# Down products that load the next part's first operand before the evictions, h before its weights, and the last retention transposes one part later

## The chip, the cores and the metric

The kernel runs on one core of one Trainium2 chip. The metric is device time in microseconds (us) of one launch; the figure before is the median of three runs. The profile is one further execution of the same program, so its times are that execution's own.

The engines are named as the profile names them: PE is TensorE (its weight loads are PEld), DVE is VectorE, ACT is ScalarE, POOL is GpSimd, and SP is the queue that issues nearly all DMAs.

## What is computed

The reference is one inference step of a two-layer encoder trunk of width 1024, over 1024 prompt frames and 32 frames of a running stream (1056 columns in all). Cut to what matters:

```python
# layer 0: retention, layer 1: gated linear attention (GLA); each followed by a ConvFFN
x = x + y_mixer          # retention: (silu(g) * o) @ w_out, o normalised per head, K = 2048
h = rmsnorm(x, norm_ffn[i])
u = h @ w_up             # 1024 -> 5632
c = conv over 3 frames of u
x = x + (silu(gate) * val) @ w_down    # K = 2816
```

and at the end a last RMSNorm. All matrices are fp32. The kernel splits each fp32 operand into a high part `hi` (rounded to the fp32r type that TensorE multiplies) and a rest `lo`, and forms each product as three matmuls: hi·hi, hi·lo, lo·hi.

## The kernel before, in words

Most large products (up, most of down, the projections of retention) are done by a seven-product Strassen scheme. What is left to the class `Down` are four plain "down" products, each `out[1024, columns] += W.T @ h` with the residual added:

- `d1r`, layer 0's retention output (`w_ro`, 16 K tiles), in four parts of 264 columns; it reads `scr_o[0]`, which retention has written to memory.
- `d1` of layer 1, GLA's output (`w_go`, 8 K tiles), in four parts of 264 columns.
- `down` of layers 0 and 1, the last 6 K tiles of `w_down` (`NF - NS`), in parts of 384, 384 and 288 columns.

A part c accumulates 8 output tiles nt in 8 PSUM banks (tile `pd`), so that all eight banks are taken while the last K tile is multiplied. For each K tile i, `load(c, kt)` fetches the weights (tile `raw`, then ACT's copy to `whi`, `kw` or `kh` at L104 and DVE's difference to `wlo`, `kw` or `kl`), and the operand h (a DMA into a room `hr`, then ACT's copy to `hh` at L1248 and DVE's difference to `hl` at L1249; in `d1r` and `d1` these rooms lie in the tiles AR and XB, so the trace calls them AR and XB). Weights of the K tiles in `keep` stay on chip for all parts, and a later part begins with them. In the plain `down` of layer 0, K tiles 0 and 1 were split early; their tiles are called `ehi` and `elo`.

After the last K tile of each bank, `evict` adds bank and residual on DVE (L1662 in `d1r`, L1728 in layer 0's `down`), squares the result on ACT (L138) and sums the squares on DVE and POOL (L149). In layer 0's `down` it also makes the next layer's operand, ACT at L153 and DVE at L154 (tile XA). The next part's products need these banks: a bank is free when its eviction has read it. During the first `hold` K tiles J of a new part only 7 of the 8 output tiles are done, so that one bank serves the norm of the part before (`norm_a`, tile `pn`).

Retention's last step, four PE transposes into a PSUM tile `pt` (L831), a product with the gate on DVE (L832) and a store to `scr_o`, is left over as a "tail" and is run by `run_tails` from within `d1r`. Its 32 columns are read by part 3 of `d1r` alone.

The order on each engine is made by a scheduler that goes by the order in which the code is written, by dependences, by its own estimate of times and by when a buffer of a pool comes free. Each engine runs its own list strictly in that order; SP issues its DMAs in its order too, and stands still while the next DMA's room is taken. The kept residual load of a part (`xr`, L1259) is a DMA of 1 MB or more on that queue.

The names that follow: h is the right operand, "residual" is `xr`, "part 0 to part 1" is the change from c = 0 to c = 1.

Of the kernel before, what the change touches and what calls it, by code (L numbers as in the profile page):

```python
# [52 lines left out]
def trunk_kernel(ctx: ExitStack, tc: tile.TileContext, io):  # L53
    nc = tc.nc
# [44 lines left out]
    def load_w(src, dst=None, after=None):  # L99
        i = uid()  # L100
        raw = raw_tile(f"raw{i}")
        nc.sync.dma_start(raw, src)
        hi, lo = dst or (w_tile(f"whi{i}"), w_tile(f"wlo{i}"))
        ins = S.copy(hi, raw), V.tensor_tensor(lo, raw, hi.bitcast(F32), op=ALU.subtract)  # L104
        if after is not None:
            for a, b in zip(ins, after):
                order(a, b)
        return hi, lo
# [3 lines left out]
    def preload(*keys):  # L112
        for k in keys:
            ahead[k] = load_w(io[k[0]][k[1:]])
# [99 lines left out]
    def new_ss(depth=1):  # L214
        return [nps[0].tile([P, 384], F32, tag="ss", name=f"ss{uid()}", bufs=2 * depth) for _ in range(2)]
# [286 lines left out]
    def pairs_phase(cs, SA, sp, UR, NB, gn, xp, finish, then):  # L502
# [77 lines left out]
        def leave(f, s):  # L580
# [7 lines left out]
            else:  # L588
# [5 lines left out]
                nc.sync.dma_start(scr_qk[key[0], key[1], :, :, c0:c0 + n].rearrange("d p t -> p d t"), u)  # L594

        load(0)
        for n, (s, f, i) in enumerate(seven_order(len(todo))):
            m = ORD[i]
            if n in (14, 18):
                t = cs[n // 4 - 3]  # L600
                V.tensor_tensor(t, t, R, op=ALU.mult)
            if s == 0 and i == 2 and f + 1 < len(todo):
                load(f + 1)
            if i == 0:
                unit[f, s] = {}
                U[f, s] = UA.tile([P, 2, 2 * TH], F32, tag="u", name="", bufs=3)

            def put(j, half, op, t, b):
                V.tensor_tensor(U[f, s][:, j, half * TH:half * TH + TH], t, b, op=op)

            seven(m, unit[f, s], W[f], X[s], sm, snap, put)
            if i == 6:
                leave(f, s)
            later(steps, 1)
            if f == len(todo) - 1 and (s, i) in then:
                then[s, i]()
# [11 lines left out]
    def retention(d1):  # L628
# [214 lines left out]
        first_down = []  # L843
        run = chunk(heads[0], 0)
        next(run)
        for n in range(len(units)):
            next(run)
            then = None
            if n + 1 < len(units):
                h, m = units[n + 1]  # L850
                if h not in heads:
                    heads[h] = Head(h)
                then = chunk(heads[h], m)
                next(then)
            next(run)
            if then is None:
                for split in first_down:
                    split()
            if n == len(units) - 4:
                for kt in range(3):  # L860
                    o = RH * P + 16 + kt * D
                    q = RH * P + 16 + 3 * D + kt * TH
                    first_down.append(d1.early(kt, raw_tile("he")[:, :TH] if kt == 2 else early[-1][:, q:q + TH],
                                               early[-1][:, o:o + D]))
            if n in (0, 2):
                refill(n + 1)
            if n == 4:
                xs[0] = sample_x(rp)
            run = then
# [331 lines left out]
    def run_tails(sm):  # L1201
        while tails:
            tails.pop()(sm)

    def later(todo, k):
        for _ in range(min(k, len(todo))):
            todo.pop(0)()
# [3 lines left out]
    class Down:  # L1211
# [23 lines left out]
        def load(self, c, kt):  # L1235
            if (c, kt) in self.ops:
                return
            c0, n = self.chunks[c]
            if kt not in self.keep:
                w = load_w(self.wsrc(kt))  # L1240
            else:
                if kt not in self.kept:
                    self.kept[kt] = load_w(self.wsrc(kt), self.room("kw"))
                w = self.kept[kt]
            hr = self.room("hr")[:, :n]
            nc.sync.dma_start(hr, self.hsrc(kt)[:, c0:c0 + n])
            hh, hl = self.room("hh"), self.room("hl")
            S.copy(hh[:, :n], hr)  # L1248
            V.tensor_tensor(hl[:, :n], hr, hh[:, :n].bitcast(F32), op=ALU.subtract)  # L1249
            self.ops[c, kt] = w, (hh, hl)  # L1250

        def run(self, room, evict, norm_a, norm_b, done, nxt=()):
            self.room = room
            nk, sm, keep = self.nk, self.sm, self.keep
            todo, ss, last = [], None, None
            for c, (c0, n) in enumerate(self.chunks):
                xr = room("xr")[:, :KT * n].rearrange("p (k t) -> p k t", k=KT)
                if c:
                    nc.sync.dma_start(xr, self.res[:, :, c0:c0 + n])  # L1259
                prev, ss = ss, new_ss()  # L1260
                kts = list(range(nk))
                if c:
                    kts = list(keep) + [k for k in kts if k not in keep]
                J = self.hold
                ps, dg = {}, [None]

                def mm(i, nt):
                    if nt not in ps:
                        ps[nt] = sm("pd")
                    k = slice(nt * P, nt * P + P)  # L1270
                    w, h = self.ops[c, kts[i]]
                    o = ps[nt][:, :n]
                    PE.matmul(o, w[0][:, k], h[0][:, :n], start=i == 0, stop=False)  # L1273
                    PE.matmul(o, w[0][:, k], h[1][:, :n], start=False, stop=False)  # L1274
                    self.last_mm = PE.matmul(o, w[1][:, k], h[0][:, :n], start=False, stop=i == nk - 1)  # L1275

                for i, kt in enumerate(kts):
                    self.load(c, kt)
                    if c == 0 and i == 4:
                        nc.sync.dma_start(xr, self.res[:, :, c0:c0 + n])  # L1280
                    if c == len(self.chunks) - 1 and i == nk - 3:
                        preload(*nxt)
                    if c == 0 and i < self.narrow:
                        for nt in range(5):
                            mm(i, nt)
                        continue

                    if c == 0 and i and i == self.narrow:
                        for nt in range(5, KT):
                            for k in range(i):  # L1290
                                mm(k, nt)

                    if prev is None or i > J:
                        for nt in range(KT):
                            mm(i, nt)
                            if i == nk - 1:
                                evict(c, nt, xr[:, nt], ps[nt][:, :n], ss)
                        if c == 0 and i == self.narrow:
                            run_tails(sm)
                        later(todo, 3 if nk > 8 else 6)  # L1300
                        continue

                    if i < J:
                        for nt in range(KT - 1):
                            mm(i, nt)
                        if i == J - 1:
                            dg[0] = norm_a(c - 1, prev)
                    else:
                        first = 5 if norm_b else 3
                        for nt in range(first):  # L1310
                            mm(i, nt)
                        if norm_b:
                            norm_b(c - 1, dg[0])
                        for k in range(J):
                            mm(k, KT - 1)
                        for nt in range(first, KT):
                            mm(i, nt)
                        todo.extend(done(c - 1, last))
                last = xr
            return ss, todo, xr  # L1320
# [594 lines left out]
```

## Time and profile before

| | us |
|---|---|
| median of 3 runs (lowest to highest) | 2878.23 (2876.97 to 2879.57) |
| profiled execution, its own time | 2871.2 |
| its span, first to last instruction | 2869.3 |
| PE busy | 2791.4 (97%) |
| DVE busy | 2145.1 (75%) |
| ACT busy | 1332.3 (46%) |
| POOL busy | 277.8 (10%) |
| `d1r`, from its first product to the start of the last L1273 | 709.5 to 910.0 |
| layer 0's `down`, likewise | 1538.0 to 1619.2 |
| `d1` of layer 1, likewise | 2046.1 to 2144.1 |
| layer 1's `down`, likewise | 2781.1 to 2853.1 |

PE works nearly all the time, so what matters is where it stands still and at what clock it runs. The last four rows are places in the span. The whole program's granted clock is 0.993 of full speed.

### The profile page before, as it was taken

The page shows a single profiled execution, that of the slowest core. Times are in us where ns is not written, and L with a number is a line of the kernel's source. Part 1 is how long each engine was busy: PE and PEld are TensorE (multiplying, and loading weights), DVE is VectorE, ACT ScalarE, POOL GpSimd, SP SyncE. Part 2 cuts the span into 40 slices and gives each one's busy share as a digit, 9 for nine tenths or more (in the row PEclk, how much of TensorE's full clock was granted, in tenths as well). Part 3 has the DMA queues.
Part 4 walks back from the last instruction along what each step waited for, and adds up shares of the span by engine and source line. Part 5 has one row for each costly group of instructions (what it writes and reads, how often), then busy time and mean ns, then how long its engine had stood idle before and what let it go on. Part 6 is the DMA issues. An engine that isn't in the chain of part 4 may idle for free.

```text
span 2869.3 us, 52602 instructions
## 1 busy us (share of the span) xinstructions
PE 2791.4 (97%) x20954; PEld 2687.3 (94%) x20954; DVE 2145.1 (75%) x3529; ACT 1332.3 (46%) x2401; POOL 277.8 (10%) x516
## 2 busy tenths in 40 slices
PE   8999999999999999999999999999998999999998
PEld 8999988788999999999999889999998999999997
DVE  7777777777678887878775577774498788878756
ACT  8433344444444544445443455553254444445434
POOL 1000000000000111111000232220011111110001
PEclk9999999999999999999999999999999999999999
DMA  6333377664765223333867201114642233428663
GB/s 219 106 124 103 128 262 239 199 192 154 260 210 166 82 75 128 121 128 113 286 205 246 90 27 46 51 44 153 222 155 70 75 110 123 143 75 271 210 231 115
DMA packets 234486, 427.22 MB, mean 149 GB/s; under 512 B 27616, under 2 KB 146016, under 8 KB 233216
## 3 DMA queue, kind: packets, MB, share of 16 engines
q1 hardware_dynamic: 233696, 423.27, 44.4%
q8 instruction: 164, 2.69, 0.4%
q14 instruction: 82, 0.67, 0.1%
q10 hardware_dynamic: 544, 0.59, 0.1%
HBM read 299.94 MB, written 123.85 MB: 148 GB/s over the span
## 4 chain that ended last, share of the span: by engine, by line
PE 80%; DVE 9%; DMA 4%; ACT 3%; issue 2%; POOL 1%; SPq 0%; DVEq 0%; ACTq 0%; POOLq 0%
PE pu L333 16%; PE pu L328 16%; PE pu L332 16%; PE pd L1274 3%; PE pd L1275 3%; PE pd L1273 3%; PE psv L233 2%; PE psv L232 2%; PE psv L231 2%; PE pj L124 1%; PE pj L126 1%; PE pj L125 1%; PE pg L124 1%; PE pg L125 1%; PE pg L126 1%
## 5 line engine op out<-in xcount | busy, mean ns | idle before, releaser
L104 DVE TENSOR_TENSOR wlo<-raw,whi 128x1024 fp32r<-128x1024 f32 x161 | 201.3, 1253 | 97.3 <-ACT whi L104 46.0
L1527 ACT COPY AR<-pu 128x264 f32<-128x264 f32 x264 | 99.0, 375 | 303.0 <-PE pu L333 300.3
L104 ACT CAST whi<-raw 128x1024 fp32r<-128x1024 f32 x161 | 167.8, 1047 | 118.4 <-DMA raw<-w_ro 26.7
L333 PE MATMUL pu<-XA,wgl 128*128 128x264 f32 x752 | 213.8, 284 | 0.0
L328 PE MATMUL pu<-XA,wgh 128*128 128x264 f32 x752 | 213.3, 284 | 0.0
L332 PE MATMUL pu<-XA,wgh 128*128 128x264 f32 x752 | 213.2, 283 | 0.0
L1274 PE MATMUL pd<-XB,whi 128*128 128x264 f32 x552 | 158.2, 288 | 2.2 <-DVE XB L1249 2.2
L1549 DVE SCALAR_TENSOR_TENSOR AR<-AR,cw 128x1058 f32<-128x1058 f32 x88 | 115.9, 1318 | 58.5 <-ACT AR L1548 55.9
L1275 PE MATMUL pd<-XB,wlo 128*128 128x264 f32 x552 | 158.3, 288 | 0.0
L1273 PE MATMUL pd<-XB,whi 128*128 128x264 f32 x552 | 154.0, 287 | 0.0
L328 PE MATMUL pu<-XA,wsh 128*128 128x264 f32 x520 | 148.7, 286 | 1.7 <-DVE AR L1523 1.0
L333 PE MATMUL pu<-XA,wsl 128*128 128x264 f32 x520 | 148.6, 286 | 0.8 <-DVE wsl L301 0.8
L332 PE MATMUL pu<-XA,wsh 128*128 128x264 f32 x520 | 147.8, 284 | 0.0
L301 DVE TENSOR_TENSOR wtl<-rv,wth 128x1024 fp32r<-128x1024 f32 x58 | 71.0, 1225 | 101.6 <-ACT wth L300 99.6
L1523 DVE TENSOR_TENSOR AR<-AR,pu 128x264 f32<-128x264 f32 (+2 forms) x440 | 144.6, 368 | 0.0
L328 PEld LDWEIGHTS pu<-XA,wgh 128*128 128x128 f32 x752 | 141.6, 188 | 0.0
L332 PEld LDWEIGHTS pu<-XA,wgh 128*128 128x128 f32 x752 | 141.5, 188 | 0.0
L333 PEld LDWEIGHTS pu<-XA,wgl 128*128 128x128 f32 x752 | 141.4, 188 | 0.0
L328 PE MATMUL pu<-XA,whi 128*128 128x264 f32 x448 | 127.5, 285 | 3.8 <-ACT XA L1418 3.0
L333 PE MATMUL pu<-XA,wlo 128*128 128x264 f32 x448 | 127.3, 286 | 1.5 <-DVE wlo L104 1.5
L332 PE MATMUL pu<-XA,whi 128*128 128x264 f32 x448 | 127.0, 285 | 0.2
L328 PE MATMUL pu<-XA,wth 128*128 128x264 f32 x408 | 116.3, 285 | 0.1
(478 smaller groups left out, 10547.1 us busy)
## 6 DMA issues: line engine op xcount, KB each, us to landing
raw<-w_ro SPq DMA_DIRECT2D x52, 512.0 KB, 4.8
rg<-w_up SPq DMA_DIRECT2D x44, 512.0 KB, 3.6
rv<-w_up SPq DMA_DIRECT2D x44, 512.0 KB, 3.5
scr_h<-AR SPq DMA_DIRECT2D x44, 512.0 KB, 2.7
AR<-scr_x SPq DMA_DIRECT2D x32, 528.0 KB, 4.9
scr_x<-AR SPq DMA_DIRECT2D x32, 528.0 KB, 3.6
raw<-scr_w SPq DMA_DIRECT2D x32, 512.0 KB, 5.2
AR<-scr_h SPq DMA_DIRECT2D x28, 528.0 KB, 4.8
```

Of the source, the lines that this page charges most:

```text
L104: ins = S.copy(hi, raw), V.tensor_tensor(lo, raw, hi.bitcast(F32), op=ALU.subtract)
L124: PE.matmul(ps, hi[:, k], rh, start=kt == 0, stop=False)
L301: V.tensor_tensor(l_, src, h.bitcast(F32), op=ALU.subtract)
L328: mm = PE.matmul(ps, wh[:, k], x[:, 0, kt], start=m in (1, 2, 4, 5) and kt == 0, stop=False, skip_group_check=True)
L332: PE.matmul(ps, wh[:, k], x[:, 1, kt], start=False, stop=False, skip_group_check=True)
L333: mm = PE.matmul(ps, wl[:, k], x[:, 0, kt], start=False, stop=kt == 3, skip_group_check=True)
L1273: PE.matmul(o, w[0][:, k], h[0][:, :n], start=i == 0, stop=False)
L1274: PE.matmul(o, w[0][:, k], h[1][:, :n], start=False, stop=False)
L1275: self.last_mm = PE.matmul(o, w[1][:, k], h[0][:, :n], start=False, stop=i == nk - 1)
L1523: V.tensor_tensor(u[:, d:d + n], t[:, o:o + n], b[:, o:o + n], op=op)
L1527: S.copy(t, b)
L1549: V.scalar_tensor_tensor(cj, uj[:, 1:T + 3], cw[:, nt, 1:2], cj, op0=ALU.mult, op1=ALU.add)
```

## The change

```diff
             c0, n = self.chunks[c]
+            hr = self.room("hr")[:, :n]
+            nc.sync.dma_start(hr, self.hsrc(kt)[:, c0:c0 + n])
             if kt not in self.keep:
                 w = load_w(self.wsrc(kt))
             ...
-            hr = self.room("hr")[:, :n]
-            nc.sync.dma_start(hr, self.hsrc(kt)[:, c0:c0 + n])
             hh, hl = self.room("hh"), self.room("hl")
...
                     self.load(c, kt)
+                    if i == nk - 1 and c + 1 < len(self.chunks):
+                        self.load(c + 1, (list(keep) or [0])[0])
...
-                        if c == 0 and i == self.narrow:
-                            run_tails(sm)
                         later(todo, 3 if nk > 8 else 6)
                         continue
                     if i < J:
                         for nt in range(KT - 1):
                             mm(i, nt)
+                        if c == 1 and i == 1:
+                            run_tails(sm)
```

Three edits, all in `Down`. `load` writes the DMA of h ahead of that of its weights. At the last K tile of a part, `load` of the next part's first K tile (a kept one) is written ahead of that last tile's products and evictions. The tail of retention is run in part 1 after the second K tile, no longer in part 0 after the fourth. Nothing is added or left out: the same instructions stand in another order. The lines below the edits are two higher in the changed kernel (L1662 is L1664 there, L1728 is L1730), and the DMA of h is L1240 there.

PE, `d1r`, end of part 0, before; `pd_7535` is output tile 4 of part 0, `pt_7630` the transposes, `on_7469` retention's last rows:

```order
L1273 MATMUL pd_7535<-XB_7516,whi_7999 128x264
L1274 MATMUL pd_7535<-XB_7516,whi_7999 128x264
L831 MATMUL pt_7630<-ident,on_7469 128x32 x4
L1275 MATMUL pd_7535<-XB_7516,wlo_8000 128x264
L1273 MATMUL pd_7576<-XB_7516,whi_7999 128x264
```

PE in the changed kernel, 52 rows later, after the second K tile of part 1 (`pd_8091` is its output tile 6):

```order
L1273 MATMUL pd_8091<-XB_7516 128x264
L1274 MATMUL pd_8091<-XB_7516 128x264
L1275 MATMUL pd_8091<-XB_7516 128x264
L831 MATMUL pt_8119<-ident,on_7469 128x32 x4
L1273 MATMUL pd_8067<-XB_7516 128x264
```

The transposes stood among the last products of part 0, with ten products of that part behind them; now they stand behind 42 products of part 1.

PE, layer 0's `down`, part 0 to part 1, before; `pd_16844` is the last bank of part 0, `pd_17070` to `pd_17094` are the seven banks of part 1, `hh_17066` and `hl_17067` the two halves of its first h:

```order
L1275 MATMUL pd_16844<-hh_16982,kl_16976 128x384
L1273 MATMUL pd_17070<-hh_17066,ehi_16674 128x384
L1273 MATMUL pd_17074<-hh_17066,ehi_16674 128x384
L1273 MATMUL pd_17078<-hh_17066,ehi_16674 128x384
L1273 MATMUL pd_17082<-hh_17066,ehi_16674 128x384
L1273 MATMUL pd_17086<-hh_17066,ehi_16674 128x384
L1273 MATMUL pd_17090<-hh_17066,ehi_16674 128x384
L1273 MATMUL pd_17094<-hh_17066,ehi_16674 128x384
L1274 MATMUL pd_17070<-hl_17067,ehi_16674 128x384
```

The same place in the changed kernel, where the first h is `hh_16987` and `hl_16988`:

```order
L1275 MATMUL pd_16844<-hh_16982,kl_16977 128x384
L1273 MATMUL pd_17070<-hh_16987,ehi_16674 128x384
L1274 MATMUL pd_17070<-hl_16988,ehi_16674 128x384
L1275 MATMUL pd_17070<-hh_16987,elo_16675 128x384
L1273 MATMUL pd_17074<-hh_16987,ehi_16674 128x384
```

and one K tile on (second h `hh_17099`, `hl_17100`; `pn_17150` is the first matmul of the norm of part 0):

```order
L1273 MATMUL pd_17090<-hh_17099,ehi_16727 128x384
L1273 MATMUL pd_17094<-hh_17099,ehi_16727 128x384
L168 MATMUL pn_17150<-ones,ss_16814 128x1
L1274 MATMUL pd_17070<-hl_17100,ehi_16727 128x384
L1275 MATMUL pd_17070<-hh_17099,elo_16728 128x384
```

Before, the seven products with the rounded half stood first in K tile 0, and those with its rest behind them; now K tile 0 goes bank by bank, and the sorting by halves has moved to K tile 1, with the first matmul of the norm in its middle.

DVE at that place, before (L1728 are evictions 3 to 7, `hl_17067` is the rest of the first h of part 1):

```order
L1728 TENSOR_TENSOR AR_7512<-AR_7512,pd_16828 128x384
L154 SCALAR_TENSOR_TENSOR XA<-AR_7512,gcol,XA 128x384
L1728 TENSOR_TENSOR AR_7512<-AR_7512,pd_16832 128x384
L154 SCALAR_TENSOR_TENSOR XA<-AR_7512,gcol,XA 128x384
L149 TENSOR_TENSOR ss_16814<-ss_16814,sq_17008 128x384
L154 SCALAR_TENSOR_TENSOR XA<-AR_7512,gcol,XA 128x384 x2
L149 TENSOR_TENSOR ss_16814<-ss_16814,sq_17028 128x384
L1728 TENSOR_TENSOR AR_7512<-AR_7512,pd_16836 128x384
L1728 TENSOR_TENSOR AR_7512<-AR_7512,pd_16840 128x384
L1728 TENSOR_TENSOR AR_7512<-AR_7512,pd_16844 128x384
L1249 TENSOR_TENSOR hl_17067<-AR_7512,hh_17066 128x384
```

DVE in the changed kernel, from eviction 3 on (L1730); `hl_16988` now stands ahead of eviction 0, and `hl_17100` follows two rows behind the last row here:

```order
L1730 TENSOR_TENSOR AR_7512<-AR_7512,pd_16828 128x384
L154 SCALAR_TENSOR_TENSOR XA<-AR_7512,gcol,XA 128x384 x2
L149 TENSOR_TENSOR ss_16814<-ss_16814,sq_17013 128x384
L154 SCALAR_TENSOR_TENSOR XA<-AR_7512,gcol,XA 128x384
L1730 TENSOR_TENSOR AR_7512<-AR_7512,pd_16832 128x384
L1730 TENSOR_TENSOR AR_7512<-AR_7512,pd_16836 128x384
L1730 TENSOR_TENSOR AR_7512<-AR_7512,pd_16840 128x384
L154 SCALAR_TENSOR_TENSOR XA<-AR_7512,gcol,XA 128x384
L149 TENSOR_TENSOR ss_16814<-ss_16814,sq_17033 128x384
L154 SCALAR_TENSOR_TENSOR XA<-AR_7512,gcol,XA 128x384
L1730 TENSOR_TENSOR AR_7512<-AR_7512,pd_16844 128x384
L154 SCALAR_TENSOR_TENSOR XA<-AR_7512,gcol,XA 128x384
```

Evictions 5 and 6 have moved ahead of two of DVE's other steps; eviction 4 and eviction 7 stand behind more of them. On ACT, the copies of the next three h (`hh_17099`, `hh_17125`, `hh_17167`) now stand in a row behind the square of output tile 3. On SP, the DMA of the first h of part 1 now stands ahead of the residual of part 1; before, it stood behind it.

## The prediction

> **What bounds the kernel now.** I read the header first, for the engine that sets the time:
>
> ```profile
> span 2869.3 us, 52602 instructions
> PE 2791.4 (97%) x20954; PEld 2687.3 (94%) x20954; DVE 2145.1 (75%) x3529; ACT 1332.3 (46%) x2401; POOL 277.8 (10%) x516
> ```
>
> PE is idle for 2869.3 − 2791.4 = 77.9 us in all. The change takes no product away, so it can win only from those idle stretches and from the clock, and lose only by making new ones. So the second view is the waits of PE, for the lines that the change touches:
>
> ```profile
> PE pt L831 <- DVE AR L1662: 2.9, 1, 2.9
> ...
> PE pd L1273 <- DVE AR L1728: 2.9, 1, 2.9
> ...
> PE pd L1274 <- DVE hl L1249: 0.5, 1, 0.5
> ```
>
> Three waits, 6.3 us: PE waits once for an eviction of `d1r` (L1662), once for one of layer 0's `down` (L1728), then for `hl`. No wait of this size stands at the other part changes of `Down`, and layer 1's products and the final down keep nearly their order, so I cost them at nothing: their cover is that PE does not stop there now.
>
> The third view is the timeline around the first wait. Columns: start, duration, engine, line, operation, and in brackets the idle time before and what ended it.
>
> ```profile
> 758.81 1.05 ACT L104 CAST whi<-raw 128x1024 fp32r<-128x1024 f32 x1 [5.27 <-DMA raw<-w_ro]
> ...
> 760.29 0.28 PE L1274 MATMUL pd<-XB,whi 128*128 128x264 f32 x1
> ...
> 761.51 0.43 DVE L1249 TENSOR_TENSOR XB<-AR,XB 128x264 fp32r<-128x264 f32 x1 [0.39 <-ACT XB L1248]
> ...
> 761.86 1.22 DVE L104 TENSOR_TENSOR wlo<-raw,whi 128x1024 fp32r<-128x1024 f32 x1
> ...
> 762.99 1.10 DVE L1662 TENSOR_TENSOR AR<-AR,pd 128x264 f32<-128x264 f32 x3
> ...
> 763.47 0.43 PE L831 MATMUL pt<-ident,on 32*128 32x32 f32 x4 [2.89 <-DVE AR L1662]
> ...
> 763.83 0.39 PE L1275 MATMUL pd<-XB,wlo 128*128 128x264 f32 x1
> ...
> 764.06 0.28 PE L1273 MATMUL pd<-XB,whi 128*128 128x264 f32 x1
> ...
> 764.18 0.28 PE L1274 MATMUL pd<-XB,whi 128*128 128x264 f32 x1
> ```
>
> The transposes `pt` need a bank, so they wait for eviction 0; that starts at 762.99, because DVE's list has weight splits (`wlo`) and splits of part 1's h (L1249) ahead of it, and these were late: ACT had waited 5.27 us for the weights' DMA. The ten last products of part 0, ready since 760.29, stand behind `pt`. So the evictions are late on account of DMA and DVE, and PE is late twice over.
>
> The fourth view is the timeline of layer 0's `down`, part 0 to part 1 (SPq is the DMA queue):
>
> ```profile
> 1547.79 0.58 SPq L1259 DMA_DIRECT2D AR<-scr_x  x1
> ...
> 1548.41 9.93 SPq L1246 DMA_DIRECT2D AR<-scr_h  x3
> ...
> 1560.35 0.51 ACT L1248 CAST hh<-AR 128x384 fp32r<-128x384 f32 x1 [3.67 <-DMA AR<-scr_h]
> ...
> 1561.28 1.59 DVE L1728 TENSOR_TENSOR AR<-AR,pd 128x384 f32<-128x384 f32 x3 [3.28 <-PE pd L1275]
> ...
> 1563.78 0.61 DVE L154 SCALAR_TENSOR_TENSOR XA<-AR,gcol,XA 128x384 fp32r<-128x384 f32 x1
> ...
> 1564.54 0.34 PE L1275 MATMUL pd<-hh,kl 128*128 128x384 f32 x1
> ...
> 1564.72 1.03 PE L1273 MATMUL pd<-hh,ehi 128*128 128x384 f32 x5
> ...
> 1565.30 0.55 DVE L149 TENSOR_TENSOR ss<-ss,sq 128x384 f32<-128x384 f32 x1
> 1565.56 0.60 ACT L153 ACTIVATE XA<-AR,gcol 128x384 fp32r<-128x384 f32 x1
> ...
> 1568.07 1.47 DVE L1728 TENSOR_TENSOR AR<-AR,pd 128x384 f32<-128x384 f32 x3
> ...
> 1568.67 0.90 PE L1273 MATMUL pd<-hh,ehi 128*128 128x384 f32 x2 [2.92 <-DVE AR L1728]
> ...
> 1569.46 0.55 DVE L1249 TENSOR_TENSOR hl<-AR,hh 128x384 fp32r<-128x384 f32 x1
> ...
> 1570.07 0.55 PE L1274 MATMUL pd<-hl,ehi 128*128 128x384 f32 x1 [0.50 <-DVE hl L1249]
> ```
>
> Seven products with `hh` need seven free banks at once. Five are free (five products in 1.03 us from 1564.72); evictions 5 to 7 come at 1568.07, since DVE's list has the next layer's operand (L154) and a sum (L149) ahead of them. Behind them comes `hl`, the 0.50.
>
> Fifth, the clock, in 3.41-us stretches (busy time of PE, PEld, DVE, ACT, POOL, then granted clock, DMA share, GB/s):
>
> ```profile
> 716.92:720.33 3.41, 1.73 (x13) 1.31 (x11) 2.29 (x3) 2.40 (x4) 0.00 (x0) 1.00 1.07 378
> 720.33:723.74 3.41, 2.79 (x12) 2.79 (x13) 1.13 (x4) 0.41 (x1) 0.00 (x0) 0.50 1.06 394
> 761.29:764.70 3.41, 1.23 (x11) 1.19 (x12) 3.19 (x8) 2.68 (x7) 0.00 (x0) 1.00 0.72 231
> 764.70:768.12 3.42, 3.42 (x17) 3.42 (x17) 2.91 (x7) 1.86 (x6) 1.52 (x2) 0.50 1.07 337
> 1566.84:1570.25 3.41, 1.07 (x3) 0.56 (x4) 3.41 (x8) 3.10 (x7) 0.49 (x1) 1.00 0.88 328
> 1570.25:1573.66 3.41, 3.41 (x12) 3.41 (x13) 3.41 (x5) 2.71 (x5) 1.66 (x2) 0.50 0.76 246
> 1618.04:1621.45 3.41, 1.73 (x13) 1.49 (x12) 3.37 (x9) 3.41 (x10) 0.72 (x1) 1.00 0.86 312
> 1621.45:1624.86 3.41, 1.67 (x9) 1.67 (x10) 3.41 (x7) 2.95 (x7) 1.13 (x2) 1.00 0.34 115
> ```
>
> PE idle for 2.18 us (3.41 − 1.23) of one stretch is followed by a stretch at 0.50, and so is 2.34 in `down`. Idle for 1.68 was followed by 0.50 once (the first pair) and by 1.00 once (the last pair), so I take 1.7 as the limit. Each of the two places loses a second time. At 1.00 a 264-column product follows the next by 0.12 us (764.06 to 764.18), so the 3.42 us at 0.50, with 15 to 17 products (the row counts 17, those at its edges among them), would be 1.8 to 2.04 us at 1.00. A tripped stretch costs some 1.4 to 1.6, I take 1.55; two places 3.1 us.
>
> The Trainium skill, "TensorE: Matmul & The Clock Gate", section "HAM oscillation — how this bites in real kernels", gives as its abstract rule "no PE-idle gaps >~3.4µs". By that rule gaps of 2.9 us would cost no clock, and removing them would bring no 3.1 us. The trace disagrees here: clock 0.50 behind 2.89 and 2.92 us of idle.
>
> **The change, part by part.**
>
> *The transposes move to part 1 (d1r, part 0 to 1).* Ten products of 0.12 us run on from 760.41, so PE reaches part 1 at about 761.6 to 761.8. There it needs the bank of eviction 0. The order on DVE has the same splits ahead of the evictions as before, so "next K tile ahead of the evictions" changes nothing at this place: h was split there already. Eviction 0 ends at 762.99 + 1.10/3 = 763.4 unchanged, or about 0.6 earlier if the h-before-weights order lets ACT take h ahead of the second weights (ACT's row at 761.74 shifted; the h copy is about 0.4 us, the split 0.43): 762.8. PE idles 1.05 to 1.6 us in place of 2.89, then perhaps 0.3 at a later bank, since the fourth to eighth evictions follow at some 0.4 each, and a bank's three products take 0.36. `pt`'s own 0.36 (763.47 to 763.83) stays, later, in part 1, where a spare bank exists and nobody waits but `scr_o`'s store, read 90 us later by part 3. At 764.18 before, PE had done two of the ten products left; after, it has done ten and some of part 1. Gain: 2.89 − 1.3 − 0.2 = **1.4**, bounds 0.9 (evictions unmoved, waits at two banks) and 2.9 (no wait).
>
> *d1r, part 2 to 3.* The order puts one `wlo` split behind the evictions that it stood ahead of:
>
> ```profile
> 859.87 1.23 DVE L104 TENSOR_TENSOR wlo<-raw,whi 128x1024 fp32r<-128x1024 f32 x1 [1.35 <-ACT whi L104]
> ...
> 861.01 1.78 DVE L1662 TENSOR_TENSOR AR<-AR,pd 128x264 f32<-128x264 f32 x5
> ...
> 861.20 0.28 PE L1275 MATMUL pd<-XB,wlo 128*128 128x264 f32 x1
> ...
> 861.58 0.36 PE L1273 MATMUL pd<-XB 128*128 128x264 f32 x1
> ...
> 869.70 0.28 PE L1275 MATMUL pd<-XB,wlo 128*128 128x264 f32 x1
> ```
>
> PE stands 0.38 − 0.12 = 0.26 between these products. Evictions that start up to 1.1 us earlier take that away: gain **0.3**, bounds 0 and 0.4. The split that is now later (1.23) is of weights that part 3 uses first at 869.70, behind the kept K tiles: 8 us of cover.
>
> *Layer 0's `down`, part 0 to 1.* K tile 0 now goes bank by bank, three products of 0.173 (0.52) each, as seven hh products no longer need seven banks at once; its `hl` stands ahead of eviction 0. From 1564.72 the seven banks are done at about 1568.35. Eviction 4 can end at about 1566.6, 5 and 6 (moved forward) at 1567.1 and 1567.6; the banks are asked for at 1566.8, 1567.3 and 1567.8, so the margin is about 0.2 at each and I count no wait. Then seven hh products of K tile 1 to 1569.55. Late next is `pn`, the norm's first matmul: it needs the sum of squares of the last output tiles, which I put at 1570.7 by laying DVE's new list end to end with the durations above (0.55 a sum, 0.61 an operand, 0.49 an eviction): 1.1 of waiting, and 0.5 more for the second `hl` (0.55, next on DVE). At 1571.2 it then stands 14 + 7 products beyond where before stood at 1570.07 (seven), so 21 products of 0.173 = 3.6 ahead, less 1.13 of later time: gain **2.5**. Bounds: 3.4 (both waits gone, 2.92 + 0.50) and 0.5 (`pn` waits 2 us more, if DVE's list slips by three of its operands).
>
> ACT's three `hh` copies in a row stand ahead of the squares of output tile 4; at 0.51 each they take 1.5 us there, contained in the 1570.7. On SP the first h passes the 1 MB residual: its landing gets earlier, and the residual (issue row 1547.79) later by one h, whose issue took at most 9.93 / 3 = 3.3 us; it is first needed at the evictions of part 1, 6 K tiles of 24 products at 0.173, or 25 us, on.
>
> *Clock.* If idle falls to at most 1.6 in one piece (place 1) and to 1.1 + 0.5 in two (place 2), both lie below 1.7: 3.1 in the profiled execution. Over other executions the stretches fall differently on the gaps. A gap of 2.89 puts over 1.7 into one stretch with a chance of (2 × (2.89 − 1.7) + 3.41 − 2.89) / 3.41 = 0.85, and with 2.18 as the limit 0.57. I take 0.8 before (1.7 is borne out by more rows, and other short idle adds), 0.1 after: 0.7 × 3.1 = **2.2**.
>
> *Sum.* Idle 1.4 + 0.3 + 2.5 = 4.2. Against the profiled execution's own time (2871.2, span 2869.3): 2871.2 − 4.2 − 3.1 = 2863.9. The median of the runs, 2878.2, is 7.0 above that execution; there I take the mean over stretches, 4.2 + 2.2 = 6.4: 2878.2 − 6.4 = **2871.8**. The limit of what can be told from no change is 0.2%, 5.8 us.
>
> **Rivals.**
>
> *The clock gives nothing* (B). Both places keep enough idle in one stretch (1.6 and 1.6 against 1.7 is close, and 1.68 tripped once). Then only idle counts: 2878.2 − 4.2 = 2874.0. Against: a stretch's edge must fall outside the whole gap, and at place 2 the two waits have products between them.
>
> The rule of the Trainium skill named above comes to the same 2874.0.
>
> *Layer 0's `down` gives it back* (C). `pn`'s wait, one instruction in the middle of PE's list with all of K tile 1 behind it, takes the place of the eviction wait: the gain there is 0.5 and its clock stays. 1.4 + 0.3 + 0.5 + 1.1 = 3.3: 2874.9. For it: DVE is busy for the whole of 3.41 us in that stretch, so anything added slips. Against: sums stood no later in its list than before.
>
> *It does not do what it says* (D). In `d1r` h was already split early, and PE at place 1 waits for the same eviction; if the ten products only move the wait behind them and place 2 shifts its wait likewise, 2877.5 to 2878.2.
>
> *Slower* (E). ACT runs its list in order, and the three `hh` copies now wait for three h DMAs, all issued behind the residual; the squares, and with them `pn` on PE, wait behind. One of these DMAs took from 1548.41 to 1560.35, 12 us, against 1565.6 at which ACT comes to it (the end of its L153 step before). It decides only if an h lands over 6.4 + 5.8 = 12.2 us after that, at 1577.8: 2884 or more. Against: before, three such DMAs were issued by 1558.34, and with 12 us from there the last is in at 1570.4, which makes case C and not this one.
>
> **How the numbers follow.** The forecast (A) 0.53, own range 2868 to 2873.5, of it 0.46 beyond 0.2% (below 2872.4) and 0.07 within; B 0.22, C 0.12, D 0.06, all within 0.2%; E 0.07, slower. So faster 0.46, within 0.2% 0.47, slower 0.07. The range for 8 in 10 goes from 2867.5 (gains at their upper bounds, 2.9 + 0.4 + 3.4, and 3.1 of clock, are 9.8, so 2868.4, and 1 us for the spread of a median) to 2876.5, which takes in A, B and C and leaves out D, E.
>
> **What would show it.** Right: the wait of `pt` gone from PE's waits, PE's idle ahead of part 1 of `d1r` at 1.0 to 1.6; in `down` the 2.92 gone and `pn` at about 1.1, `hl` at 0.5; clock 1.00 in the stretches behind both places. Wrong: clock 0.50 behind either place (B), `pn` at 3 us or more (C), idle at place 1 of over 2.5 (D), ACT's `hh` copies waiting for DMA beyond 1570 (E).

## The result, and the profile after

| | us |
|---|---|
| before, median of its runs beside the changed kernel | 2878.9 |
| changed, median of 4 runs (lowest to highest) | 2863.03 (2859.14 to 2868.11) |
| ratio, 95% interval | 0.9941 [0.9917, 0.9965] |
| changed, measured again with the experiments (e5): median, ratio | 2861.54, 0.9949 [0.9936, 0.9962] |
| changed, profiled execution: its own time, span | 2868.1, 2866.2 |

The change is faster by 0.5 to 0.6%, some 15 to 17 us by the two ratios; the forecast was 6.4 us, and 2863.0 lies below its range. The direction was right, the size was not: of the 8 to 11 us that were missed, 4.4 (in the profiles) to 5.2 (in whole runs) lie at a place that the prediction had not looked at.

The profiled executions hide this: their spans differ by 3.1 us alone (2869.3 and 2866.2). At the four places of the table further below the changed one gains 11.4 us, but between equal products of PE it spent 3.2 us more in retention, ahead of every edit (products 2800 to 4000, counted from the program's first: 250.0 and 253.2), 2.2 more at the end of `d1r` (5600 to 6000: 51.9 and 54.1) and 2.7 more early in GLA (11600 to 12000: 47.9 and 50.6). A second execution of the changed kernel (e5) has 251.3, 51.9 and 47.9 there, so most of this is not the change's. The header and PE's waits of the changed kernel:

```profile
span 2866.2 us, 52610 instructions
PE 2791.4 (97%) x20954; PEld 2688.0 (94%) x20954; DVE 2143.0 (75%) x3529; ACT 1331.8 (46%) x2401; POOL 277.3 (10%) x516
```

```profile
PE pd L1273 <- DVE AR L1664: 1.2, 2, 1.0
...
PE pn L168 <- DVE ss L149: 1.1, 1, 1.1
```

The 2.9 of `pt`, the 2.9 of `down` and the 0.5 of `hl` are gone; 1.0 (the longer of the two waits in the first row) and 1.1 stand in their place. But one more row of before is gone, which stood third in the same list and was not used, since its line is not in the diff:

```profile
PE pj L124 <- DVE AR L1728: 3.4, 1, 3.4
```

`pj` is the first product of GLA, the phase behind layer 0's `down`. Its place in the timeline, before (PE's last product of `down` at 1619.47, the three last evictions, `pj`):

```profile
1619.40 0.45 DVE L1728 TENSOR_TENSOR AR<-AR,pd 128x288 f32<-128x288 f32 x1
1619.47 0.29 PE L1275 MATMUL pd<-hh,kl 128*128 128x288 f32 x1
...
1622.33 1.17 DVE L1728 TENSOR_TENSOR AR<-AR,pd 128x288 f32<-128x288 f32 x3
...
1623.19 0.44 PE L124 MATMUL pj<-XA,whi 128*128 128x384 f32 x1 [3.42 <-DVE AR L1728]
```

and after:

```profile
1615.33 0.45 DVE L1730 TENSOR_TENSOR AR<-AR,pd 128x288 f32<-128x288 f32 x1
...
1616.12 0.45 DVE L1730 TENSOR_TENSOR AR<-AR,pd 128x288 f32<-128x288 f32 x1
1616.19 0.29 PE L1275 MATMUL pd<-hh,kl 128*128 128x288 f32 x1
1616.62 0.45 PE L124 MATMUL pj<-XA,whi 128*128 128x384 f32 x1
```

Evictions 0 to 4 come early and 5 to 7 some 3 us later, in both. Before, `pj` starts within the second group, after in step with eviction 4. No engine's order differs here, so what `pj` waits for must differ. The built program tells which PSUM bank each tile gets (output tile nt of the last part of `down`, then the two `pj`):

```
            nt  0  1  2  3  4  5  6  7    pj
before          1  4  5  2  7  6  0  3    0, 1
changed         1  4  5  2  0  7  6  3    0, 1
```

`pj` lies in bank 0 in both. That bank held output tile 6 before, and holds tile 4 now. In the built program before, the tail's `pt` takes bank 0 in `d1r`, between two parts, and every later part has its first three tiles in banks 7, 6, 0; in the changed one `pt` takes bank 1, and they stand in 0, 7, 6. It is so still in `down`, 850 us later.

Layer 0's `down`, part 0 to 1, after: evictions 4 to 6 at 1566.81, then `pn` waits for the sum of squares:

```profile
1566.81 1.47 DVE L1730 TENSOR_TENSOR AR<-AR,pd 128x384 f32<-128x384 f32 x3
...
1571.19 0.55 DVE L149 TENSOR_TENSOR ss<-ss,sq 128x384 f32<-128x384 f32 x1
1571.66 1.01 DVE L1249 TENSOR_TENSOR hl<-AR,hh 128x384 fp32r<-128x384 f32 x2
1571.79 0.38 PE L168 MATMUL pn<-ones,ss 128*128 128x1 f32 x2 [1.14 <-DVE ss L149]
```

`d1r`, part 0 to 1, after (the last `wlo` ahead of the evictions, the evictions, PE):

```profile
763.85 1.23 DVE L104 TENSOR_TENSOR wlo<-raw,whi 128x1024 fp32r<-128x1024 f32 x1
...
764.99 1.78 DVE L1664 TENSOR_TENSOR AR<-AR,pd 128x264 f32<-128x264 f32 x5
...
765.47 0.40 PE L1273 MATMUL pd<-XB 128*128 128x264 f32 x1 [0.96 <-DVE AR L1664]
```

And the clock in the stretches at both places, 1.00 throughout where before had 0.50 behind them:

```profile
762.80:766.21 3.41, 2.45 (x21) 2.24 (x20) 3.30 (x7) 2.82 (x5) 0.00 (x0) 1.00 0.59 196
766.21:769.63 3.42, 3.42 (x28) 3.21 (x27) 2.92 (x8) 1.93 (x7) 1.51 (x2) 1.00 0.97 286
1568.35:1571.76 3.41, 2.30 (x14) 1.98 (x12) 3.40 (x7) 3.41 (x7) 1.11 (x1) 1.00 0.93 310
1571.76:1575.17 3.41, 3.30 (x19) 3.21 (x20) 3.41 (x5) 2.12 (x4) 1.02 (x1) 1.00 0.61 190
```

### The profile page after: what moved, and what is told of

It reads as the page before. It is cut to its first block, busy times and chain, and to the rows that moved or that the text cites. A ratio compares the mean times of both kernels' runs of the same rounds, so it can differ in the third digit from the quotient of the medians.

```text
span 2866.2 us, 52610 instructions
## 1 busy us (share of the span) xinstructions
PE 2791.4 (97%) x20954; PEld 2688.0 (94%) x20954; DVE 2143.0 (75%) x3529; ACT 1331.8 (46%) x2401; POOL 277.3 (10%) x516
## 4 chain that ended last, share of the span: by engine, by line
PE 80%; DVE 8%; DMA 5%; ACT 3%; issue 2%; POOL 1%; SPq 0%; DVEq 0%; ACTq 0%; POOLq 0%
PE pu L333 16%; PE pu L328 16%; PE pu L332 16%; PE pd L1274 3%; PE pd L1275 3%; PE pd L1273 3%; PE psv L233 1%; PE psv L232 1%; PE psv L231 1%; PE pj L124 1%; PE pj L126 1%; PE pj L125 1%; PE pl L990 1%; PE pg L124 1%; PE pg L125 1%
```

## The experiments

Two theories stood against each other: "banks" (the tail's move rotates the banks, and this ends `pj`'s wait) and "loads" (the h loads bring `down` forward, and `pj`'s wait goes with it). The two halves of the change were run apart, and then the bank alone.

**e1, the third edit alone.**

```diff
-                        if c == 0 and i == self.narrow:
-                            run_tails(sm)
...
+                        if c == 1 and i == 1:
+                            run_tails(sm)
```

> The kernel before with the third edit alone (the retention tail in part 1 of d1r). The built program shows the banks of PSUM that each tile gets: as in the changed kernel, the three banks 0, 7, 6 of every later part stand in the order 0, 7, 6 and no longer 7, 6, 0, so that GLA's first product pj (bank 0) asks for the bank of output tile 4 of the last part of layer 0's down, not of tile 6. Theory 'banks': both the wait of pt (2.89, some 1.0 left) and that of pj for an eviction (3.42 in the profile before) go: 1.9 + 3.2 of idle and some 2 x 0.8 x 1.55 = 2.5 of clock, 7.6 us, ratio 0.9974; pj without a wait over 0.5, the 2.92 wait in layer 0's down unchanged. Rival 'loads' (pj's wait went because the h loads brought the down products forward): pj still waits 3.4; 1.9 + 1.2 = 3.1 us, ratio 0.9989.

Ratio 0.9981 [0.9972, 0.9991], 5.5 us: the time decides nothing, as the interval takes in both theories (0.9974 and 0.9989). The trace does: `pj` starts without a wait that the list shows, in step with eviction 4, and the 2.92 in `down` stands. "Banks" holds:

```profile
1615.45 0.45 DVE L1728 TENSOR_TENSOR AR<-AR,pd 128x288 f32<-128x288 f32 x1
...
1615.95 0.45 PE L124 MATMUL pj<-XA,whi 128*128 128x384 f32 x1
```

In `d1r` PE waited longer than that theory had (some 1.0 left):

```profile
756.51 1.05 ACT L104 CAST whi<-raw 128x1024 fp32r<-128x1024 f32 x1 [5.05 <-DMA raw<-w_ro]
...
759.57 1.22 DVE L104 TENSOR_TENSOR wlo<-raw,whi 128x1024 fp32r<-128x1024 f32 x1
...
760.70 1.78 DVE L1662 TENSOR_TENSOR AR<-AR,pd 128x264 f32<-128x264 f32 x5
...
761.18 0.39 PE L1273 MATMUL pd<-XB 128*128 128x264 f32 x1 [4.03 <-DVE AR L1662]
```

PE ran through its ten products and then waited 4.03 us for the same eviction. In this execution PE was early and the weights were not.

**e2, the first and second edit alone** (h's DMA ahead of its weights, and the next part's first K tile loaded ahead of the last products).

> The kernel before with the first and second edit (h ahead of weights, next part's first K tile ahead of the last products) and the tail at its old place. Banks as in the kernel before. Theory 'banks': the 2.92 + 0.50 in layer 0's down become some 1.1 (pn), 2.3 of idle and some 1.2 of clock, with 0.3 to 0.5 in d1r part 2 to 3: 3.9 us, ratio 0.9986; pj still waits about 3.4 for its bank, pt about 2.9 or up to 0.6 less. Rival 'loads': pj's wait goes here: 3.9 + 3.2 + 1.2 = 8.3 us, ratio 0.9971.

Ratio 0.9982 [0.9972, 0.9992], 5.2 us. `pn` waits 1.1, `pj` 3.4, `pt` 3.4. "Loads" expected 8.3 us, which lies outside the interval (0.9971), if only just; the wait that stands in the trace decides against it. What `pj`'s wait does to the clock:

```profile
1612.82:1616.23 3.41, 1.43 (x11) 1.20 (x9) 3.38 (x8) 3.41 (x10) 1.00 (x1) 1.00 0.81 292
1616.23:1619.64 3.41, 1.97 (x6) 1.97 (x7) 3.41 (x7) 2.94 (x7) 0.84 (x1) 0.50 0.38 131
1619.64:1623.06 3.42, 3.42 (x13) 3.42 (x12) 2.35 (x4) 0.04 (x1) 1.93 (x3) 0.50 0.50 159
```

Here the wait put 1.98 us of idle into one stretch and 1.44 into the next; that next stretch and the one behind it were at 0.50. In the profiled execution before, the same wait was cut into 1.68 and 1.74, and its clock cost nothing.

**e3, the bank alone**: the kernel before, with `pj` in another bank.

```diff
         pp = es.enter_context(pool("gps", space=PSUM))
+        V.memset(pp.tile([P, 3 * P], F32, tag="lv", name="pz_lv", bufs=2)[:, :1], 0.0)
+        V.memset(pp.tile([P, GDV], F32, tag="v", name="pz_v", bufs=2)[:, :1], 0.0)
```

> The kernel before, nothing of the change, with two one-column memsets on tiles of GLA's PSUM pool written ahead of its first product, so that pj lies in banks 4 and 5 (output tiles 1 and 2 of the last down part) in place of 0 and 1. Theory 'banks': the 3.42 wait of pj is gone with all else unchanged: 3.2 of idle and 1.2 of clock, 4.4 us, ratio 0.9985. Rival 'loads': pj waits as before, ratio 1.0000.

Ratio 0.9982 [0.9971, 0.9992], 5.2 us with nothing of the change in it. `pj` starts at 1620.65 without a wait, just behind the last product, with only the first five evictions begun:

```profile
1620.45 0.45 DVE L1730 TENSOR_TENSOR AR<-AR,pd 128x288 f32<-128x288 f32 x1
...
1620.65 0.34 PE L124 MATMUL pj<-XA,whi 128*128 128x384 f32 x1
```

(An L-number is up to five higher in kernels with lines added.) The waits of `pt` and in `down` stand.

**e4, the reverse**: the changed kernel, with a third such memset on the tag `ou`, which puts `pj` into bank 6, output tile 6.

> The changed kernel with three one-column memsets on GLA's PSUM pool, so that pj lies in bank 6 (output tile 6 of the last down part, as before the change by order of release) in place of bank 0. Theory 'banks': the wait of pj for an eviction comes back, 3.0 to 3.5 us, and with it 1.2 of clock: the gain over the kernel before shrinks from some 12 to some 7.5 us, ratio 0.9974. Rival 'loads': no wait, ratio as the changed kernel's, 0.994 to 0.996.

Ratio 0.9979 [0.9969, 0.999]; the changed kernel has 0.9949 [0.9936, 0.9962], and the intervals do not meet. The wait is back:

```profile
1617.90 1.17 DVE L1733 TENSOR_TENSOR AR<-AR,pd 128x288 f32<-128x288 f32 x3
...
1618.76 0.69 PE L124 MATMUL pj<-XA,whi 128*128 128x384 f32 x1 [3.42 <-DVE AR L1733]
```

So the bank is shown from both sides: whether `pj` asks for the bank of output tile 4 or of tile 6 decides over a wait of 3.4 us. The two ratios differ by 8.7 us (about 4 to 13), a range that takes in the 4.6 that the wait's place shows in the table below; in its profile e4 also spent 3.8 us more in part 0 to 1 of `d1r` than e5, long ahead of the memsets. How much of the rest is the bank's is open.

**e5, the changed kernel once more.**

> The changed kernel again, unaltered. Theory 'banks': its gain is the sum of the parts, e1 (1 - 0.9981) and e2 (1 - 0.9982): ratio 0.9963, 10.6 us, with pj without a wait, pn at 1.1, and at d1r part 0 to 1 an idle stretch between 1 and 4 us that differs from execution to execution. Rival 'more': there is a gain beyond the parts, and the first comparison's 0.9941 (17 us) holds.

0.9949 [0.9936, 0.9962], 14.7 us (10.9 to 18.4): between the two expectations, the sum of the parts (0.9963) just outside the interval. The parts' own intervals are some 0.001 wide to each side, so whether there is a gain beyond them isn't settled.

**e6, the second edit alone.**

```diff
                     self.load(c, kt)
+                    if i == nk - 1 and c + 1 < len(self.chunks):
+                        self.load(c + 1, (list(keep) or [0])[0])
```

> The kernel before with the second edit alone (next part's first K tile split ahead of the last products and evictions); h still behind the weights, tail at its old place, banks as before. Theory 'order of the products': PE's new order in layer 0's down hangs on this edit; the 2.92 + 0.50 become some 1.1 at pn, 0.3 to 0.5 in d1r part 2 to 3 stays out if it hangs on the first edit; 3.5 us, ratio 0.9988, pj still waits 3.4. Rival 'h ahead of its weights': hh of the next K tile comes late without the first edit, the wait stays at 2 us or more, ratio 1.0000.

0.9976 [0.9966, 0.9987], 6.9 us, where 3.5 was expected and the interval starts at 3.7; `pn` at 1.1, `pj` at 3.4. The second edit alone carries what happens in `down`.

**e11, the first edit alone.**

> The kernel before with the first edit alone (h's DMA ahead of its weights). Layer 0's down keeps its order on PE and its 2.92 and 0.50. Theory: what goes is the 0.5 of d1r part 2 to 3, which e6 without this edit did not have (segment of 560 products 69.2 to 69.4 without, 68.7 with): ratio 0.9998, the same within 0.001. Rival: h ahead of the weights carries part of the gain at other places: ratio 0.998 or less.

1.0004 [0.9994, 1.0014]: no difference that can be measured. Its 0.6 us is in the trace (the table below) and nowhere else.

**e7, a small residual in `d1r`.** DVE holds the evictions back with splits of weights whose DMAs stand behind the residual of part 1. Is it the residual?

```diff
                 if c:
-                    nc.sync.dma_start(xr, self.res[:, :, c0:c0 + n])
+                    few = 1 if c == 1 and self.narrow else KT
+                    nc.sync.dma_start(xr[:, :few], self.res[:, :few, c0:c0 + n])
+                    if few < KT:
+                        G.memset(xr[:, few:], 0.0)
```

> The changed kernel, with the residual of d1r's part 1 loaded for one of eight output tiles only (the other seven are set to zero by POOL), so 135 KB in place of 1.08 MB stand ahead of the weights on the DMA queue; the sum of these columns is left incomplete. Theory 'late weights': the weights that DVE splits ahead of the evictions land some 3 us earlier, and the idle stretch ahead of part 1 of d1r falls below 0.6 us; ratio 0.9955 to 0.996. Rival 'PE waits for the evictions themselves' (DVE's order sets it, not the DMA): idle stays at 1 us or more, ratio as e5.

This kernel leaves seven of eight tiles of that residual out of the sum, so only its times are of use. 0.9938 [0.9925, 0.9952], and the idle stretch was 3.34: the theory of the residual fell. The last split ahead of the evictions belongs to weights that came at 758.4, residual or not:

```profile
758.46 1.04 ACT L104 CAST whi<-raw 128x1024 fp32r<-128x1024 f32 x1 [0.93 <-DMA raw<-w_ro]
...
760.19 1.22 DVE L104 TENSOR_TENSOR wlo<-raw,whi 128x1024 fp32r<-128x1024 f32 x1
...
761.33 1.78 DVE L1667 TENSOR_TENSOR AR<-AR,pd 128x264 f32<-128x264 f32 x5
761.81 0.39 PE L1276 MATMUL pd<-XB 128*128 128x264 f32 x1 [3.34 <-DVE AR L1667]
```

**e8, the residual's load at the third K tile.**

```diff
-                if c:
-                    nc.sync.dma_start(xr, self.res[:, :, c0:c0 + n])
...
-                    if c == 0 and i == 4:
+                    if i == (4 if c == 0 else 2):
                         nc.sync.dma_start(xr, self.res[:, :, c0:c0 + n])
```

> The changed kernel with the load of a part's residual written at its third K tile, no longer at its start. In the built program only layer 0's down and the final down move: K tile 1 of part 1 goes bank by bank too, with pn behind it. Theory: the 1.14 wait of pn goes or falls under 0.4 and nothing else moves: 1 us less than e5, ratio 0.0004 below it. Rival: what is late is the sum of squares on DVE and whoever needs the banks, so the wait moves to an eviction or to hl, no difference to e5.

0.9952 [0.9939, 0.9966]. The `pn` wait is gone, and that stretch of `down` is 1.6 us shorter (table), but whole runs can't tell it from e5.

**e9, the evictions first on DVE**, and **e10**, e8 and e9 together.

```diff
-                w = load_w(self.wsrc(kt))
+                w = load_w(self.wsrc(kt), after=self.ev if self.nk > 8 and c else None)
...
-                                evict(c, nt, xr[:, nt], ps[nt][:, :n], ss)
+                                self.ev = evict(c, nt, xr[:, nt], ps[nt][:, :n], ss)
```

(`load_w` orders the `wlo` split behind `after`.)

> The changed kernel; in d1r the difference splits (wlo) of a part's own weights are ordered behind the last eviction of the part before, on DVE alone and without a semaphore. In the built program PE's order is that of the changed kernel; DVE's list at d1r part 0 to 1 has three wlo behind the evictions that stood ahead of them, and these weights' raw tiles come free later. Theory 'DVE's list': the idle stretch ahead of part 1 (0.96, 2.39, 3.08 in three executions of this order, 3.34 with the small residual) falls below 0.4 us, 1.5 to 2.5 us of gain and some 1 us of clock; ratio about 0.9940. Rival 'the weights come back later': the three weights are wanted some 8 us on and their splits and next loads are now late, PE waits at a wlo of part 1 for 1 us or more: ratio 0.995 or above.

> The changed kernel with e8's later residual and e9's order on DVE together. If both gains hold: no idle over 0.4 at d1r part 0 to 1, no pn wait in layer 0's down, ratio e9 less 0.0004. If e9's rival holds: as e8, 0.995.

0.9973 [0.9963, 0.9983] and 0.997 [0.996, 0.998]: both probably slower than the changed kernel (the interval of e5 ends at 0.9962, that of the first comparison at 0.9965, so they all but meet). e9:

```profile
763.18 0.41 ACT L1248 CAST XB<-AR 128x264 fp32r<-128x264 f32 x1 [6.44 <-DMA AR<-scr_or]
...
763.62 0.43 DVE L1249 TENSOR_TENSOR XB<-AR,XB 128x264 fp32r<-128x264 f32 x1 [6.39 <-ACT XB L1248]
763.97 1.78 DVE L1664 TENSOR_TENSOR AR<-AR,pd 128x264 f32<-128x264 f32 x5
764.45 0.39 PE L1273 MATMUL pd<-XB 128*128 128x264 f32 x1 [1.73 <-DVE AR L1664]
```

With the weights' splits out of the way, the evictions wait for the split of an h, whose DMA is as late. In e10 h came in time and that idle was gone; but in both PE waited 2.8 and 2.7 us for the norm of part 0 further on (`rm`, L207). The order alone isn't shown to be the cause: with the changed kernel's own order on DVE in `d1r`, e5 has no such wait there, but e8 has 0.81 and e4 1.75. What holds is that the lateness moved and didn't go; the rival of e9's expectation was right in that, though it had looked for the wait at a `wlo`.

**All profiles side by side.** The time between the starts of two PE products, counted from the program's first (the count is the same in all; idle and clock are both in it). Places: `d1r` part 0 to 1 (products 4400 to 4860), part 2 to 3 (5000 to 5560), `down` part 0 to 1 (10840 to 11260), `down` to GLA (11260 to 11440), in us.

| kernel | d1r 0 to 1 | d1r 2 to 3 | down 0 to 1 | down to GLA |
|---|---|---|---|---|
| before | 66.21 | 69.18 | 72.67 | 29.69 |
| e11 first edit | 66.18 | 68.71 | 72.54 | 31.24 |
| e6 second edit | 65.20 | 69.39 | 68.48 | 29.69 |
| e2 first and second | 64.98 | 68.68 | 68.49 | 32.12 |
| e3 bank alone | 66.34 | 69.27 | 72.55 | 26.00 |
| e1 third edit | 64.45 | 69.32 | 73.73 | 26.42 |
| changed | 62.76 | 68.68 | 68.49 | 26.42 |
| e5 changed again | 62.92 | 68.66 | 68.47 | 26.40 |
| e4 changed, late bank | 66.69 | 68.68 | 68.49 | 31.02 |
| e8 changed, residual later | 62.65 | 68.70 | 66.87 | 26.35 |
| e7 changed, small residual | 64.18 | 68.71 | 68.48 | 26.41 |
| e9 changed, evictions first | 64.75 | 70.03 | 68.48 | 26.40 |
| e10 e8 and e9 together | 64.09 | 70.35 | 66.83 | 26.36 |

The third column falls wherever the second edit is (72.9 in the mean to 68.5, and to 66.9 and 66.8 in e8 and e10: 4.4 without these two), the second wherever the first is (69.3 to 68.7: 0.6; e9 and e10 lose it again), the last wherever `pj`'s bank comes free early (30.8 to 26.3: 4.4). The first column goes from 65.8 (tail in part 0, five rows) to 63.9 (five rows, without e7, e9 and e10), 1.9, with rows of both kinds that overlap. It takes in the start of `d1r`, ahead of the place in question, which varies by 3.6 us among all kernels; from product 4560 to 4900 the same rows go from 47.3 (46.1 to 48.6) to 45.8 (43.5 to 48.7), 1.5. The sum is some 11 us (10.9 to 11.3), at the lower end of what e5 measured (14.7, 10.9 to 18.4). What the rest is, if there is one, stays open.

## Why the prediction was wrong

- *The list of places.* This is the step that failed. "It can win only from those idle stretches", and the waits read "for the lines that the change touches": of 77.9 us of idle the row of 3.4 on `pj` was left out, so that place stood in the sum at nothing, because neither its line nor any engine's order there changed. The change did reach it, through the bank that `pj` stands in. The stretches of this very wait stood in the prediction, as 1.68 and 1.74 us of idle that did not trip the clock, and served only as a limit. Worth 4.4 us in the profiles, 5.2 in e3.
- *Layer 0's `down`.* Mechanism and size held: `pn` at 1.1 forecast, 1.14 measured; 2.5 us forecast without the clock, and 2.6 measured (the three rows with one stretch at 0.50, before, e11 and e3, have 72.6 in the mean against 68.5, and 1.55 of the 4.1 is the clock's). Only the 0.5 for the second `hl` did not come: no wait on `hl` stands among PE's waits.
- *`d1r`, part 0 to 1.* Gain 1.4 forecast without the clock, 1.5 to 1.9 with the clock in it measured. But the picture of an idle stretch of 1.0 to 1.6 was too firm: with the tail moved it was 0.88, 0.96, 2.38, 3.08 and 4.03 us in five executions (e8, changed, e5, e4, e1), and with the tail in part 0 it was 2.89 to 5.07 in five (before, e3, e11, e2, e6). PE now arrives earlier, but eviction 0 starts when DVE has split the late weights, 23.2 to 26.3 us behind product 4560 in all ten. So the 2.89 that the prediction started from was the smallest of its kind, and that the means agree is partly luck.
- *`d1r`, part 2 to 3.* 0.3 forecast, 0.6 measured, and it hangs on the first edit.
- *The clock.* That both places lose a second time was right for `down`: 0.50 behind it in before, e1, e3 and e11, 1.00 in all nine executions with the second edit in the table. At `d1r` the clock loss did not go with the change: e1, e5 and e7 still had a stretch at 0.50 there (from 761.8, 763.8 and 763.0), where a chance of 0.1 was given. The rule of the Trainium skill ("TensorE: Matmul & The Clock Gate", "HAM oscillation — how this bites in real kernels"), "no PE-idle gaps >~3.4µs", is contradicted again by e5, where a gap of 2.38 us, 1.90 of it in one stretch, was followed by the 0.50 from 763.8.
- *Rivals.* B to E all lie above the measured time. ACT's three `hh` copies (E) did not wait for DMA: in the changed kernel they run at 1566.48.

With the third place at 4.4, `down` at 4.4, and `d1r` at 1.9 + 0.6, the same working would have given 2878.2 − 11.3 = 2866.9. The 4 us from there to the measured 2863.0 are not accounted for.

## What to carry to other kernels

A tile that is moved or allocated at another time can hand every later tile another PSUM bank: list the banks before and after, beside the order, and check every wait on an eviction in the whole program, not only at the lines of the diff. Where a new phase begins, put its first product into a bank that is evicted first; two one-column memsets did that here for 5 us. Ahead of an eviction, an entry of DVE's list that waits for a DMA became a wait of PE here; taking one out did not help, since the next one was as late (e7, e9). And compare a wait over several executions before it is put into a sum: the one in `d1r` was 2.9 us in the first profile and 3.2 to 5.1 in four others with the tail at its old place.

## What the runs showed of the hardware

The same idle time does not always cost clock. `pj`'s wait of 3.42 to 3.43 us stands in five executions, cut differently by the 3.41-us stretches of the clock:

| execution | idle in the two stretches, us | stretches at 0.50 that followed | `down` to GLA, us |
|---|---|---|---|
| before | 1.68, 1.74 | 0 | 29.69 |
| e6 | 1.82, 1.61 | 0 | 29.69 |
| e11 | 1.40, 2.03 | 1 | 31.24 |
| e4 | 2.99, 0.43 | 1 | 31.02 |
| e2 | 1.98, 1.44 | 2 | 32.12 |

Without the wait that place takes 26.3 us, so one and the same wait cost 3.4 to 5.8 us. A profile of one execution can so show little more than half of its price, and a median over runs, in which the stretches fall differently, should lie between the two. No sharp limit comes out: 1.82 us of idle in a stretch was free here, while 1.75 in e4 (from 775.2) was followed by 0.50.
